# The context's norm, projections and delta rule beside the two feed-forwards

## The chip, the cores and the metric

The kernel runs on one core of one Trainium2 chip. The metric is the device time of one execution in microseconds (us). Matrix work runs on TensorE (PE in the profile, its weight loads PEld), elementwise work on VectorE (DVE) and ScalarE (ACT), a little on GpSimd (POOL); SyncE (SP) issues the DMAs. TensorE writes only to PSUM, which has eight banks of 128 x 512 float32.

## The reference

Two blocks on 256 tokens of width 1024, all in float32.

The first block has two layers. Each is a mixer (three branches, attention of two sorts and a convolution, gated and summed) and a feed-forward of width 4096:

```
h = rms_norm(x, g_ffn)
x = x + square(relu(h @ w_ff1)) @ w_ff2
```

The second block takes that x and a context of 256 tokens. Both are normalised, modulated by factors computed from two conditioning vectors, and multiplied by the same `w_in`. What matters here is that the context's part does not need x:

```
zx = modulate(rmsnorm(x,   g), mod_x) @ w_in     # needs the first block
zc = modulate(rmsnorm(ctx, g), mod_c) @ w_in     # does not
k_all, v_all = concat(kc, kx), concat(vc, vx)    # differential attention of qx
_, = wkv_scan(0, scan_c) -> s_ctx                # a delta rule over the context's 256 steps
y  = wkv_scan(s_ctx, scan_x)                     # and over x's, from the state it left
s = s * w - (s @ kk) (kk * a)^T + v k^T          # one step, per head, in two directions
```

The two branches are merged, and an expert stage (16384 experts, top 16 of 8 heads) follows.

## The kernel before

A matmul in float32 is made of three in the `fp32r` form: each operand is split into a high part (`wh`, `hh`, on ScalarE, line 304) and a low part (`wl`, `hl`, on VectorE, line 269), and lines 325 to 327 or 343 to 345 multiply high by high, low by high and high by low. Weights come by DMA as 128 x 1024 pieces (128 x 512 in the second block) into `raw`. A *unit* is 256 output columns of a projection: `linA_unit` gives them transposed, channels on the partitions, `linB_unit` tokens on the partitions; either is 48 matmuls of 256 columns. `bank()` hands out a PSUM bank: of `psa` (three) by default, `psw` (two) or `psr` (three) inside a `stream`, or the one bank of `psm` where the stream is `single`.

The stages, in the profile's time: mixer of layer 0, its feed-forward (313 to 512), mixer of layer 1, its feed-forward (819 to 1013), the second block (1013 to 1931), the experts. `layer()` holds mixer and feed-forward; both take their tiles from one pool, `layer`. The feed-forward runs 16 tiles: `f1` of tile i (line 893), relu and square (895 to 898), `f2` of tile i - 1 into four accumulating banks. At its last tile but one of layer 1 it computes the context's norm (`ctx_norm`) into `hh`, `hl`, and after the tiles the unit `zw` of the context (`w_proj`), of which the context uses one half of the columns.

`mods_stream` computes the modulation factors from the conditioning vectors in three rounds of eight steps; five steps run at the start of each feed-forward, and the first round, which the norms need, is complete there in layer 0 (line 1003).

`second()` then goes through this order of work:

```
z_proj(context): zk, zv, 8 units -> DRAM      front(context, half 0), back(context, half 0)
front(context, half 1); bk and bv of the context, 8 units; keys to DRAM
x to DRAM; norm of x; zw, zk, zv, zr of x     back(context, half 1), front(x, half 0)
bq, bk, bv, bg of x                           back(x, half 0), front(x, half 1)
attention                                     back(x, half 1); merges, output, norm
```

`wkv_front` makes, for half the heads, the decays (line 1231), the products of keys (line 1270), and inverts 32 x 32 triangular blocks on VectorE, going out to DRAM and back on both sides (`din`, `dout`; lines 1279 to 1303); its last part (1316, 1323) makes what the back takes. `wkv_back` carries the state S through eight groups of 32 steps (lines 1346, 1362, 1374). Their tiles come from two rotating sets: `w4` with 8 buffers and `w8` with 9. A front of the context takes 6 of `w8`, one of x 8 or 6.

What sets the order: each engine works through one queue in order. The queues are written at build time by a planner that simulates the program's timeline; among what is ready it prefers what stands earlier in the program, and `high_priority(offset=30000)` puts fronts and backs ahead of the projections. A tile that takes memory of another waits until the other is no longer used; this holds for the buffers of a rotating set and for a pool opened where another was closed.

Of the kernel before, what the change touches and what calls it, by code (L numbers as in the profile page):

```python
# [194 lines left out]
class Kern:  # L195
    def __init__(self, tc, A, flat_at, const_at, pack_at, out):
        self.tc, self.nc, self.A, self.at = tc, tc.nc, A, flat_at
        self.const_at, self.pack_at, self.out = const_at, pack_at, out
        self.n = 0
        self.ev = 0  # L200
        self.sfx, self.single = "", False
        self.every = 3
        self.last = None
        self.late = {}
        self.held = []
        self.wide = 2048
        self.piece = 1024

# [100 lines left out]
    def pieces(self, name, piece=None):  # L309

        off, n = self.at[name]
        piece = piece or self.piece
        raw = None if self.wide < n else self.load(name)
# [47 lines left out]
    def linA_unit(self, name, hh, hl, nk):  # L361
# [4 lines left out]
        for wh, wl in self.pieces(name):  # L366
            wh = wh.rearrange("p (j k c) -> p j k c", k=kk, c=128)
            wl = wl.rearrange("p (j k c) -> p j k c", k=kk, c=128)
            for i in range(wh.shape[1]):
# [4 lines left out]
                if k == 0:  # L374
                    m += 1
                    if m % 2 == 0:
                        yield ps
# [87 lines left out]
    def layer(self, l, pool):  # L465
# [5 lines left out]
        P = {k: pk[:, a:b] for k, (a, b) in at.items()}  # L471
# [407 lines left out]


        hh = self.t(self.work, [128, 8, T], "hh", F32R)
        hl = self.t(self.work, [128, 8, T], "hl", F32R)
        self.normT(self.halves(self.x), P["g_ffn"], hh, hl, spare="t")
        self.mods_units(5, self.last)
        with self.stream("t"):
            pw = [self.bank_pair(), [self.score_bank(), self.score_bank()]]
        prev = None
        for i in range(17):
# [13 lines left out]
            if i == 15 and l and self.more:  # L902
                self.ctx_front = self.ctx_norm(pool, "TG")
# [3 lines left out]
        if l and self.more:  # L907
            self.w_proj(pool, 0, *self.ctx_front)
        self.add_x(pw)

# [67 lines left out]
    def mods_stream(self):  # L978
# [10 lines left out]
        for r in range(3):  # L989
            ps = self.t(self.psm, [128, 512], "m")  # L990
            for k in range(8):
                for q in range(4):
                    if q % 2 == 0:
                        raw = self.t(self.lpool, [128, 1024], ("qk", "TG")[k % 2], bufs=4)
# [92 lines left out]
    def v_unit(self, pool, i, hh, hl, dst, kt):  # L1087
        a = self.t(pool, [128, 2, 256], "d2", bufs=4)
# [11 lines left out]
    def ctx_norm(self, pool, tag):  # L1100

        x = [self.t(pool, [128, D], tag, bufs=4) for t in range(2)]
        for t in range(2):
            self.nc.sync.dma_start(x[t], self.A["ctx"][128 * t:128 * t + 128])
        hh, hl = [self.t(self.work, [128, 8, T], n, F32R) for n in ("hh", "hl")]
        self.mod_norm(x, self.P2["norm1_g"], 0, 1, hh, hl)
        return hh, hl

    def w_proj(self, pool, src, hh, hl):
# [4 lines left out]
        for ps in self.linA_unit("zw0", hh, hl, 8):  # L1114
# [10 lines left out]
    def z_proj(self, pool, src, hh, hl, zd):  # L1125

        nc = self.nc
        for half in range(2):
            for n, base in (("zk", 8), ("zv", 16), ("zr", 0)):
                if n == "zr" and src == 0:  # L1130
                    continue
                for i in (2 * half, 2 * half + 1):
                    for ps in self.linA_unit(f"{n}{i}", hh, hl, 8):
                        o = self.t(pool, [128, 2, T], "d2", bufs=4)
# [195 lines left out]
    def wkv_back(self, state, S, od=None):  # L1330
# [92 lines left out]
        if self.dbg is not None:  # L1423
            nc.sync.dma_start(self.dbg["o_bx"].rearrange("(m p) t -> p m t", p=128)[:, m0:m0 + 4], o)
# [99 lines left out]
    def second(self, pool, xd):  # L1524
        nc, P = self.nc, self.P2
        self.rows2 = self.t(pool, [128, 384], "rows2")
        nc.sync.dma_start(self.rows2, self.A["rows2"].partition_broadcast(128))
        self.resets = self.t(pool, [128, 264], "resets")
# [9 lines left out]
        nc.vector.tensor_scalar(self.tmka, P["rw_k_a"], -1.0, 2.0, op0=ALU.mult, op1=ALU.add)  # L1538
        dram = lambda shape, name: self.t(self.dram, shape, name)
        kTd, qTd, vd = dram([128, 8, 512], "kTd"), dram([128, 8, T], "qTd"), dram([128, 4, 1024], "vd")  # L1540
        zc, zx = dram([128, 24, T], "zc"), dram([128, 24, T], "zx")
# [29 lines left out]
        back(st, S[:, 1])  # L1571
# [249 lines left out]
def body(tc, A, flat_at, const_at, pack_at, pk2_at, out, stop=None, dbg=None, skip=0):  # L1821
    nc = tc.nc
    with ExitStack() as ctx:
        K = Kern(tc, A, flat_at, const_at, pack_at, out)
        K.pk2_at, K.dbg = pk2_at, dbg
        K.setup(ctx)
        K.n4, K.n8 = 8, 9
# [5 lines left out]
        K.wad = K.t(K.dram, [128, T], "wad")  # L1833
        K.mods_pool = ctx.enter_context(pool("mods", bufs=1))
        pk = K.t(K.mods_pool, [128, A["pk2"].shape[1]], "pk2")
        K.P2 = {k: pk[:, a:b] for k, (a, b) in pk2_at.items()}
        with pool("xp", bufs=1) as K.xp:
# [5 lines left out]
            K.psa = ctx.enter_context(pool("psa", bufs=3, space=PSUM))  # L1843
# [3 lines left out]
            with pool("psm", bufs=1, space=PSUM) as K.psm, pool("psb1", bufs=2, space=PSUM) as K.psb:  # L1847
                with pool("small1", bufs=1) as K.small, pool("mtmp", bufs=1) as K.mtmp, pool("stage1", bufs=2) as K.stage, pool("late1", bufs=1) as late, pool("layer", bufs=1) as p:
                    K.late = {n: late for n in ("pk", "rows", "TG", "mt", "OT", "OL")}
                    K.tmp = p, [128, 512], "mt", F32, 4  # L1850
                    K.lpool, K.mstream, K.more = p, K.mods_stream(), stop is None or stop > 2
                    if skip < 2:
# [77 lines left out]
```

## Time and profile before

| | |
|---|---|
| median of 3 runs | 2844.91 us (2844.22 to 2846.0) |
| the profiled execution | 2839.05 us |
| its span, first to last instruction | 2837.1 us |
| TensorE busy | 2637.1 us, 93% |
| VectorE busy | 1977.8 us, 70% |
| ScalarE busy | 1424.6 us, 50% |
| DMA queue of SyncE | 50.4% of 16 engines' span |
| granted TensorE clock, mean | 0.939 of 2.4 GHz |

Times in the profile are counted from the first instruction, so the stages can be told by them. Busy time of TensorE is modelled, as matmuls are pipelined: a matmul's duration is longer than the distance to the next one, and busy shares of a stage say more than sums of durations. A group of instructions is named by its line, engine, operation and tiles, `out<-in`; many lines are those of helpers that all stages share.

### The profile page before, as it was taken

What the parts mean: (1) busy time and instruction counts of PE and PEld (TensorE: products, weight loads), DVE (VectorE), ACT (ScalarE), POOL (GpSimd) and SP (SyncE); (2) the same over time, 40 slices, a digit from 0 to 9 for tenths busy, and PEclk for the clock granted to TensorE, in tenths of its full rate; (3) what the DMA queues carried; (4) which work ended last, traced back from release to release, by engine and by line L of the source; (5) the groups of instructions that cost most, each with busy time, mean ns of one, the idle gap of its engine ahead of it and who ended that gap; (6) DMA issues with size and microseconds to landing.
All of it is one profiled execution on the core that took longest, in us unless ns stands there. A gap on an engine that the chain in (4) does not pass through costs nothing. (4 is left out here: it accounts for less than half of the span.)

```text
span 2837.1 us, 55078 instructions
## 1 busy us (share of the span) xinstructions
PE 2637.1 (93%) x21880; PEld 2314.7 (82%) x21880; DVE 1977.8 (70%) x4104; ACT 1424.6 (50%) x2417; POOL 13.1 (0%) x36
## 2 busy tenths in 40 slices
PE   7999999999999998899789785798989999999999
PEld 7987688898679997888777454688989998888887
DVE  6986555598675577887777766476886765666666
ACT  5554444555454455665454553345445654444444
POOL 0000000000000000000000000000000000000000
PEclk9999999999999998999897766599999999999999
DMA  5534755554376654644544212064554346666665
GB/s 189 181 140 142 285 194 189 169 168 142 119 259 189 189 190 133 180 150 144 157 130 141 84 37 80 12 207 159 182 182 145 124 142 203 207 216 214 210 216 185
DMA packets 214738, 467.16 MB, mean 165 GB/s; under 512 B 53072, under 2 KB 86608, under 8 KB 213968
## 3 DMA queue, kind: packets, MB, share of 16 engines
q1 hardware_dynamic: 214480, 463.64, 50.4%
q8 instruction: 172, 2.82, 0.4%
q14 instruction: 86, 0.70, 0.1%
HBM read 425.54 MB, written 38.01 MB: 163 GB/s over the span
## 5 line engine op out<-in xcount | busy, mean ns | idle before, releaser
L269 DVE TENSOR_TENSOR wl<-raw,wh 128x1024 fp32r<-128x1024 f32 (+2 forms) x726 | 732.4, 1013 | 379.2 <-ACT wh L304 370.6
L304 ACT ACTIVATE wh<-raw 128x1024 fp32r<-128x1024 f32 (+2 forms) x726 | 642.5, 890 | 691.5 <-PE a L326 316.2
L325 PE MATMUL a<-hh,wh 128*128 128x256 f32 x2784 | 797.8, 287 | 17.3 <-ACT wh L304 9.6
L327 PE MATMUL a<-hh,wl 128*128 128x256 f32 x2784 | 796.6, 287 | 9.1 <-DVE wl L269 8.8
L326 PE MATMUL a<-hl,wh 128*128 128x256 f32 x2784 | 794.5, 286 | 2.2 <-DVE hl L269 2.2
L325 PEld LDWEIGHTS a<-hh,wh 128*128 128x128 f32 x2784 | 533.8, 192 | 29.7 <-ACT wh L304 14.3
L327 PEld LDWEIGHTS a<-hh,wl 128*128 128x128 f32 x2784 | 533.0, 192 | 20.7 <-DVE wl L269 15.3
L326 PEld LDWEIGHTS a<-hl,wh 128*128 128x128 f32 x2784 | 533.6, 192 | 8.7 <-DVE hl L269 2.4
L344 PE MATMUL a<-wl,hh 128*128 128x256 f32 (+2 forms) x640 | 195.9, 307 | 15.6 <-DVE wl L269 15.1
L344 PE MATMUL b<-wl,ah 128*128 128x512 f32 x512 | 200.8, 392 | 0.0
L343 PE MATMUL a<-wh,hh 128*128 128x256 f32 (+2 forms) x640 | 192.9, 306 | 7.9 <-DVE hl L387 6.7
L343 PE MATMUL b<-wh,ah 128*128 128x512 f32 x512 | 191.1, 393 | 3.1 <-issue 3.1
L345 PE MATMUL b<-wh,al 128*128 128x512 f32 x512 | 192.0, 392 | 0.0
L345 PE MATMUL a<-wh,hl 128*128 128x256 f32 (+2 forms) x640 | 191.8, 301 | 0.0
L344 PEld LDWEIGHTS a<-wl,hh 128*128 128x128 f32 x640 | 127.0, 198 | 27.4 <-DVE wl L269 18.2
L260 ACT ACTIVATE w<-a 32x512 f32<-32x512 f32 (+1 forms) x168 | 99.3, 592 | 98.3 <-PE a L1362 43.2
L343 PEld LDWEIGHTS a<-wh,hh 128*128 128x128 f32 x640 | 127.7, 199 | 15.7 <-DVE hl L387 7.3
L1775 ACT ACTIVATE ah<-pact 128x256 fp32r<-128x256 f32 x128 | 52.7, 412 | 171.6 <-PE b L344 159.0
L345 PEld LDWEIGHTS a<-wh,hl 128*128 128x128 f32 x640 | 126.8, 198 | 4.0 <-issue 1.0
L269 DVE TENSOR_TENSOR wl<-rawv,wh 128x1024 fp32r<-128x1024 f32 x84 | 101.8, 1223 | 38.6 <-ACT wh L304 38.6
L269 DVE TENSOR_TENSOR al<-pact,ah 128x256 fp32r<-128x256 f32 x128 | 53.1, 423 | 89.8 <-ACT ah L1775 89.7
L827 DVE SCALAR_TENSOR_TENSOR z<-U,pk,z 128x256 f32<-128x256 f32 x240 | 114.9, 479 | 0.8
(515 smaller groups left out, 4325.7 us busy)
## 6 DMA issues: line engine op xcount, KB each, us to landing
raw<-in_flat SPq DMA_DIRECT2D x266, 512.0 KB, 4.3
raw<-in_peer SPq DMA_DIRECT2D x172, 512.0 KB, 3.9
raw<-in_flat SPq DMA_DIRECT2D x276, 256.0 KB, 3.5
rawv<-in_peer SPq DMA_DIRECT2D x84, 512.0 KB, 4.6
TG<-in_flat SPq DMA_DIRECT2D x28, 512.0 KB, 5.5
qk<-in_flat SPq DMA_DIRECT2D x24, 512.0 KB, 5.2
parked<-act SPq DMA_DIRECT2D x89, 128.0 KB, 2.0
pact<-parked SPq DMA_DIRECT2D x89, 128.0 KB, 4.2
```

The source lines that it names most:

```text
L260: nc.scalar.activation(out, in_, AF.Copy, scale=1.0 if scale is None else scale)
L269: self.nc.vector.tensor_tensor(out, a, b, op=ALU.subtract)
L304: self.nc.scalar.activation(h, src, AF.Copy)
L325: mm(ps, wh[:, k], xh[:, k], start=first and k == 0, stop=False)
L326: mm(ps, wh[:, k], xl[:, k], start=False, stop=False)
L327: mm(ps, wl[:, k], xh[:, k], start=False, stop=last and k == nk - 1)
L343: mm(ps, xh[:, k], wh[:, k], start=first and k == 0, stop=False)
L344: mm(ps, xh[:, k], wl[:, k], start=False, stop=False)
L345: self.last = mm(ps, xl[:, k], wh[:, k], start=False, stop=last and k == nk - 1)
L827: nc.vector.scalar_tensor_tensor(cv[:, c], U[:, c, k_:k_ + T], wd[:, k_:k_ + 1], cv[:, c], op0=ALU.mult, op1=ALU.add)
L1775: nc.scalar.activation(ah, act, AF.Copy)
```

## The change

The context's work leaves the second block, all but the keys of its attention (`bk`).

- `layer()` is cut in two: `mixer()` and `ffn()`, and each of the four gets a pool of its own, opened where the one before is closed. What has to last from mixer to feed-forward (`pk`, `rows`, `TG`, `mt`, `OT`, `OL`) was in a pool beside them already.
- In the first feed-forward, after its norm and the modulation's steps and ahead of its tiles in the program, `ctx_proj` computes the context's norm into two `w8` tiles, copies it to DRAM (`hcd`), and computes half of `zw`, the 8 units `zk` and `zv`, and the 4 units `bv`, with tiles of 128 x 1024.
- In each feed-forward, ahead of its tiles and at high priority, one half of the context's delta rule: `wkv_front` and `wkv_back` with 5 `w4` and 6 `w8` buffers, its PSUM banks `m` and `x` in turn, and its final S sent to DRAM (`Sd`).
- `psa` has two banks, `psx` one. Where `spare_bank` is set, the default stream takes `psx` at every third call; during the feed-forwards it is left to the delta rule, and the tiles have the two of `psa`.
- The modulation's weights come into `TG` (4 buffers) alone, no longer into `qk` and `TG`.
- The second block loads S and, during the last tiles of the second feed-forward, the context's `hh` and `hl` from DRAM. Its order begins with `bk` of the context (into a `w8` tile), x's norm, `zw` and z of x, and the rest of the context's keys; then `front(x, half 0)`. `w4` and `w8` have 8 and 9 buffers there as before.

```diff
     def bank(self):
+        if self.single == "c":
+            self.turn += 1
+            return self.t(*((self.psm, [128, 512], "m"), (self.psx, [128, 512], "x"))[self.turn % 2])
         if self.single:
             return self.t(self.psm, [128, 512], "m")
+        if not self.sfx and self.spare_bank:
+            self.turn += 1
+            if self.turn % 3 == 0:
+                return self.t(self.psx, [128, 512], "x")
...
+    def ffn(self, l, pool):
...
-        self.normT(self.halves(self.x), P["g_ffn"], hh, hl, spare="t")
+        self.normT(self.halves(self.x), self.P["g_ffn"], hh, hl, spare="t")
         self.mods_units(5, self.last)
+        self.spare_bank = False
+        if l == 0:
+            self.ctx_proj(pool)
+        with self.stream("n", "c"), self.tc.high_priority(offset=30000):
+            self.n4, self.n8 = 5, 6
+            tg = self.t(pool, [128, D], "TG", bufs=4)
+            self.wkv_consts(pool, tg[:, T:T + 264])
+            wa = tg[:, :T]
+            nc.sync.dma_start(wa, self.wad)
+            S = self.t(pool, [128, 2, 4, 64], "S")
+            nc.gpsimd.memset(S, 0.0)
+            self.wkv_back(self.wkv_front(pool, 0, l, self.zc, wa), S)
+            nc.sync.dma_start(self.Sd[l], S)
...
-            if i == 15 and l and self.more:
-                self.ctx_front = self.ctx_norm(pool, "TG")
+            if i == 15 and l:
+                self.ctx_front = [self.t(self.work, [128, 8, T], n, F32R) for n in ("hh", "hl")]
+                for n in range(2):
+                    nc.sync.dma_start(self.ctx_front[n].bitcast(F32), self.hcd[:, n])
...
-        if l and self.more:
-            self.w_proj(pool, 0, *self.ctx_front)
+        self.spare_bank = True
         self.add_x(pw)
+
+    def ctx_proj(self, pool):
+
+        nc = self.nc
+        x = [self.t(pool, [128, D], "TG", bufs=4) for t in range(2)]
+        for t in range(2):
+            nc.sync.dma_start(x[t], self.A["ctx"][128 * t:128 * t + 128])
+        hh, hl = [self.t(pool, [128, 8, T], "w8", F32R, bufs=6) for n in range(2)]
+        self.mod_norm(x, self.P2["norm1_g"], 0, 1, hh, hl)
+        for n, h in enumerate((hh, hl)):
+            nc.sync.dma_start(self.hcd[:, n], h.bitcast(F32))
+        self.w_proj(pool, 0, hh, hl)
+        self.z_proj(pool, 0, hh, hl, self.zc, "mt")
+        for i in range(4):
+            self.v_unit(pool, i, hh, hl, self.vd, 0, "mt")
...
     def second(self, pool, xd):
...
-        nc.gpsimd.memset(S, 0.0)
+        for hf in range(2):
+            nc.sync.dma_start(S[:, hf], self.Sd[hf])
...
-        wac = self.t(pool, [128, T], "wa0")
-        nc.sync.dma_start(wac, self.wad)
-        self.z_proj(pool, 0, hh, hl, zc)
...
-        st = front(0, 0, zc, wac)
-        back(st, S[:, 0])
-        st = front(0, 1, zc, wac)
-        a = self.t(self.xp, [128, 2, 16, 64], "xn", bufs=1)
+        self.n4, self.n8 = 8, 9
+        a = self.w8(pool, [128, 2, 16, 64])
         fc = self.da_front(pool, a, "bk", hh, hl)
-        for i, _ in enumerate(self.da_tail(pool, fc, self.rows2[:, 64:128], False, kTd, 0)):
-            self.v_unit(pool, i, hh, hl, vd, 0)
...
         self.z_proj(pool, 1, hh, hl, zx)
-        back(st, S[:, 1])
+        for _ in self.da_tail(pool, fc, self.rows2[:, 64:128], False, kTd, 0):
+            pass
         st = front(1, 0, zx, wax)
...
-            K.psa = ctx.enter_context(pool("psa", bufs=3, space=PSUM))
+            K.psa = ctx.enter_context(pool("psa", bufs=2, space=PSUM))
+            K.psx = ctx.enter_context(pool("psx", bufs=1, space=PSUM))
...
+                    for l in range(2):
+                        with pool(f"mixer{l}", bufs=1) as p:
+                            K.mixer(l, p)
+                        with pool(f"ffn{l}", bufs=1) as p:
+                            K.ffn(l, p)
```

`wkv_consts` holds the few constants of the delta rule that `second()` made; `w_proj` takes only the first half of the `zw` weights where its source is the context.

## Rows read from the trace of the kernel before

**Rows 1.** The page's first part: busy time of each engine over the span.
```profile
PE 2637.1 (93%) x21880; PEld 2314.7 (82%) x21880; DVE 1977.8 (70%) x4104; ACT 1424.6 (50%) x2417; POOL 13.1 (0%) x36
```

**Rows 2.** Busy time by stage; after POOL the granted clock, DMA share, GB/s.
```profile
core 0: us, PE busy (x) PEld busy (x) DVE busy (x) ACT busy (x) POOL busy (x), PEclk, DMA share, GB/s
313.00:512.00 199.00, 195.34 (x1238) 166.56 (x1237) 107.89 (x137) 92.20 (x115) 0.00 (x0) 1.00 0.62 217
819.00:1013.00 194.00, 188.65 (x1223) 166.24 (x1222) 116.24 (x176) 100.97 (x135) 0.00 (x0) 1.00 0.62 199
1013.00:1931.00 918.00, 777.71 (x9357) 669.00 (x9355) 659.42 (x1533) 474.29 (x931) 8.05 (x18) 0.83 0.41 127
1013.00:1540.00 527.00, 472.70 (x5773) 431.89 (x5771) 405.89 (x946) 289.58 (x525) 5.05 (x15) 0.93 0.51 156
1540.00:1700.00 160.00, 130.58 (x1224) 88.90 (x1224) 110.44 (x257) 91.11 (x222) 1.10 (x2) 0.68 0.21 63
1700.00:1842.00 142.00, 95.95 (x1832) 76.42 (x1835) 78.76 (x207) 50.48 (x108) 0.00 (x0) 0.61 0.17 46
1931.00:2837.00 906.00, 880.47 (x5847) 805.35 (x5846) 613.26 (x1183) 443.44 (x623) 0.62 (x1) 0.99 0.56 184
```

**Rows 3.** Single lines, in stretches: ns min/median/max, first and last start in us.
```profile
L1374 PE MATMUL a<-w,w x256: 218/218/268, 1206.4 to 1325.7; 64*64 64x64 f32 x128
...
L1374 PE MATMUL a<-w,w x256: 218/218/365, 1408.9 to 1509.5; 64*64 64x64 f32 x128
...
L1374 PE MATMUL a<-w,w x224: 218/311/367, 1594.8 to 1694.0; 64*64 64x64 f32 x112
...
L1374 PE MATMUL a<-w,w x224: 311/311/366, 1775.2 to 1826.2; 64*64 64x64 f32 x112
...
L1164 ACT ACTIVATE w<-w x4: 1044/1047/1057, 1057.0 to 1590.4; 128x1024 f32<-128x1024 f32 x4
...
L1164 ACT ACTIVATE w<-w x2: 1047/1052/1057, 1198.3 to 1405.9; 128x1024 f32<-128x1024 f32 x2
...
L1270 PE MATMUL a<-w,w x256: 211/219/240, 1243.7 to 1327.5; 64*64 64x32 f32 x128
...
L1270 PE MATMUL a<-w,w x256: 218/218/267, 1451.5 to 1526.1; 64*64 64x64 f32 x128
```

**Rows 4.** The timeline inside the second feed-forward: start and duration in us.
```profile
989.74 0.28 PE L327 MATMUL a<-hh,wl 128*128 128x256 f32 x1
...
990.09 0.28 PE L327 MATMUL a<-hh,wl 128*128 128x256 f32 x1
```

**Rows 5.** Groups of TensorE between 1013 and 1931, shapes kept apart: busy us, mean ns.
```profile
L1362 PE MATMUL a<-w,w 32*32 32x64 f32 x1024 | 63.0, 255 | 41.1 <-DMA w<-dout 21.7 <-DVE w L266 13.4 <-DVE w L1303 5.1
L1323 PE MATMUL a<-w,w 32*32 32x64 f32 x1024 | 40.2, 234 | 5.2 <-ACT w L260 4.6 <-issue 0.5
L1374 PE MATMUL a<-w,w 64*64 64x64 f32 x960 | 37.4, 263 | 8.2 <-ACT w L260 8.1
...
L1223 PE MATMUL a<-wa,wup 64*128 64x256 f32 x64 | 19.3, 424 | 0.4 <-ACT w L1228 0.4
...
L1270 PE MATMUL a<-w,w 64*64 64x32 f32 x512 | 15.3, 232 | 3.8 <-DVE w L263 3.7
L1346 PE MATMUL a<-S,w 64*32 64x64 f32 x512 | 14.0, 221 | 4.4 <-DVE S L263 3.4 <-DVE w L263 1.0
```

**Rows 6.** Groups of VectorE: splits at 313 to 512 and at 1134 to 1200.
```profile
L269 DVE TENSOR_TENSOR wl<-raw,wh 128x1024 fp32r<-128x1024 f32 x63 | 77.2, 1226 | 82.3 <-ACT wh L304 82.2
...
L269 DVE TENSOR_TENSOR wl<-raw,wh 128x512 fp32r<-128x512 f32 x27 | 18.4, 687 | 2.7 <-ACT wh L304 2.5
```

**Rows 7.** Single lines again: modulation, the first feed-forward's tiles, attention.
```profile
L1003 PE MATMUL m<-ident,mt x12: 272/273/332, 325.8 to 831.9; 128*128 128x128 f32 x12
...
L895 ACT ACTIVATE mt<-a x16: 578/582/582, 337.8 to 504.7; 128x512 f32<-128x512 f32 x16
...
L1448 PE MATMUL a<-d,dq x64: 589/1057/1220, 1540.7 to 1688.8; 64*128 64x512 f32 x64
```

**Rows 8.** DMA issues: how many, KB each, median us to landing.
```profile
zc<-d SPq DMA_DIRECT2D x8, 256.0 KB, 4.1
```

More of the change, by code (lines that the diff above doesn't have):

```diff
@@ L207, in __init__ @@
         self.piece = 1024
+        self.turn, self.spare_bank = 0, True
     def uid(self, s):
@@ L359, in linB_unit, with linA_unit @@
         return ps
-    def linA_unit(self, name, hh, hl, nk):
+    def linA_unit(self, name, hh, hl, nk, one=False):
         ps = None
@@ L365, in linA_unit @@
         m = k = 0
-        for wh, wl in self.pieces(name):
+        for wh, wl in self.pieces(name, part=128 * nk if one else None):
             wh = wh.rearrange("p (j k c) -> p j k c", k=kk, c=128)
@@ L375, in linA_unit @@
                     m += 1
-                    if m % 2 == 0:
+                    if m % 2 == 0 or one:
                         yield ps
@@ L462, in rope_rows, with mixer @@
         self.add(v, v, tmp)
-    def layer(self, l, pool):
+    def mixer(self, l, pool):
         nc, C = self.nc, self.C
@@ L470, in layer @@
         nc.sync.dma_start(pk, self.A[f"pk{l}"])
-        P = {k: pk[:, a:b] for k, (a, b) in at.items()}
+        P = self.P = {k: pk[:, a:b] for k, (a, b) in at.items()}
         rw = self.t(pool, [128, 320], "rows")
@@ L1113, in w_proj @@
         sg = self.t(pool, [128, T], "sgd") if src else None
-        for ps in self.linA_unit("zw0", hh, hl, 8):
+        for ps in self.linA_unit("zw0", hh, hl, 8, one=src == 0):
             self.shifted(wa, ps[:, 0], 24)
@@ L1818, in peer_experts, with body @@
                 nc.sync.dma_start(out[:, t, c], o)
[L1821 removed]
+def body(tc, A, flat_at, const_at, pack_at, pk2_at, out):
     nc = tc.nc
@@ L1833, in body @@
         K.wad = K.t(K.dram, [128, T], "wad")
+        K.zc = K.t(K.dram, [128, 24, T], "zc")
+        K.vd = K.t(K.dram, [128, 4, 1024], "vd")
+        K.hcd = K.t(K.dram, [128, 2, 8, T], "hcd")
+        K.Sd = [K.t(K.dram, [128, 2, 4, 64], f"Sd{n}") for n in range(2)]
         K.mods_pool = ctx.enter_context(pool("mods", bufs=1))
@@ L1847, in body @@
             with pool("psm", bufs=1, space=PSUM) as K.psm, pool("psb1", bufs=2, space=PSUM) as K.psb:
-                with pool("small1", bufs=1) as K.small, pool("mtmp", bufs=1) as K.mtmp, pool("stage1", bufs=2) as K.stage, pool("late1", bufs=1) as late, pool("layer", bufs=1) as p:
+                with pool("small1", bufs=1) as K.small, pool("mtmp", bufs=1) as K.mtmp, pool("stage1", bufs=2) as K.stage, pool("late1", bufs=1) as late:
                     K.late = {n: late for n in ("pk", "rows", "TG", "mt", "OT", "OL")}
-                    K.tmp = p, [128, 512], "mt", F32, 4
-                    K.lpool, K.mstream, K.more = p, K.mods_stream(), stop is None or stop > 2
-                    if skip < 2:
-                        for l in range(2 if stop is None else min(2, stop)):
-                            K.layer(l, p)
-                    if stop is None or stop > 2:
-                        for _ in K.mstream:
-                            pass
-                    if skip == 2:
-                        K.ctx_front = K.ctx_norm(p, "TG")
-                        K.w_proj(p, 0, *K.ctx_front)
+                    K.tmp = late, [128, 512], "mt", F32, 4
+                    K.lpool, K.mstream = late, K.mods_stream()
+                    for l in range(2):
[3 more added lines that the diff above has]
+                            K.ffn(l, p)
+                    for _ in K.mstream:
+                        pass
             K.late = {}
@@ L1863, in body @@
             K.stage = stage2.enter_context(pool("stage2", bufs=2, side="right"))
[L1864 to L1874 removed]
+            with pool("psr2", bufs=3, space=PSUM) as K.psr:
+                with pool("small2", bufs=1) as K.small, pool("late2", bufs=1) as late, pool("second", bufs=1) as p:
+                    K.late = {"d2": late}
+                    K.tmp = p, [128, 512], "d2", F32, 4
+                    K.nraw, K.nsplit, K.every, K.wide, K.piece = 6, 4, 1 << 30, 1024, 512
+                    K.second(p, xd)
+                    hh = K.t(K.work, [128, 8, T], "hh", F32R)
+                    hl = K.t(K.work, [128, 8, T], "hl", F32R)
+                    K.mod_norm(K.halves(K.x), K.P2["norm2_g"], 3, 0, hh, hl, spare="w")
             K.late = {}
@@ L1877, in body @@
             psw.close()
-            if stop is not None:
-                stage2.close()
-                nc.sync.dma_start(out.rearrange("(t p) d -> p t d", p=128), K.x)
-                return
             nc.sync.dma_start(x3d, K.x)
```

55 lines of the change are left out of this document (19 added, 36 removed).

## The prediction

> **What bounds the kernel now.** I read the page's first lines, then the busy time by stage, then where the chain of the four delta-rule passes starts and stops. TensorE is busy 2637 of 2837 us, 93% [rows 1], so work can hardly be hidden: what moves to another place costs TensorE time there. The stages show where TensorE's time is poor. In the two feed-forwards (313 to 512 and 819 to 1013) the granted clock is 1.00 and 195.3 of 199 and 188.7 of 194 us are busy. From 1013, the end of the second feed-forward, to 1931, where the expert stage starts, 777.7 of 918 us are busy: 140 idle, and the clock is 0.93 in the part with the projections (1013 to 1540) and 0.68 and 0.61 after it. The last stage, 880 of 906 busy at 0.99, is left alone by the change [rows 2].
>
> Why those 918 us are poor: four passes of the delta rule (`wkv_front`, then `wkv_back`; context half 0, context half 1, x half 0, x half 1) hang on one another. Line 1374, which only a back has, runs at 1206 to 1326, 1409 to 1510, 1595 to 1694 and 1775 to 1826; the fronts begin between 1057 and 1590, the third at 1406. The second half of a front (from line 1270 on) stands still until the back before it gives up its `w8` buffers: line 1270 is drawn out from 1244 to 1327, where the first back ends at 1326, and from 1452 to 1526, where the second ends at 1510 [rows 3]. So the four are one chain, and projections lie beside only its first part.
>
> **What moves.** Eight units `zk` and `zv` and four `bv`, 48 matmuls each; half of `zw` (24; the other half is computed today and not used); one norm; two passes. A 256-column matmul is issued every 0.117 us in the feed-forward (three in 0.35) [rows 4].
> - z: 384 x 0.117 = 45 us; v: 192 x 0.117 = 22; `zw` 3; the norm's 32 transposes 3. All in the first feed-forward: 73.
> - TensorE for one context pass: 7.7 and 7.0 (half of the two forms with 512 instructions, lines 1270 and 1346, that only the context has) and a quarter of lines 1362 (63.0), 1323 (40.2), 1374 (37.4) and 1223 (19.3, and as much for 1224): 59.5 [rows 5]. Small matmuls overlap in the array and part of these rows ran at the low clock; some smaller groups are left out. I take 58, with 45 and 70 as the ends.
> - VectorE: a pass is at most what 1013 to 1540 shows: 406 us [rows 2] less some 200 splits of 512 columns at 0.69 us [rows 6] = 268, for two and a half passes: 107. First feed-forward: 108 + 25 splits at 1.23 [rows 6] = 31 + 15 for the shifts + 107 = 261 of some 350 us; second 116 + 107 = 223 of 268. ScalarE, 92 and 101 [rows 2], is lower. The DMAs (12.5 MB of weights, the turns through DRAM) find the queue at 0.62. I cost all this at nothing beside TensorE; where that cover fails, it is the late pass of rival 3.
>
> **First feed-forward.** TensorE: 199 + 73 + 58 = 330. Stalls: where passes and projections are mixed today, 54 of 527 us are idle [rows 2], 10%, with two and a half passes in them; for one pass in 330 I take 6%, 20 us (bounds 0 and 33). Growth 73 + 58 + 20 = 151. Is the pass in time? The modulation's last transposes come at 326; the norm takes about 16 (the feed-forward's own, with its first 48 matmuls, fills 313 to 338); `zw` and four z units 26 [rows 7]; out to DRAM and back two DMAs of 4 us [rows 8]: the front starts at 376. A front took 149 (1057 to 1206), a back 101 to 120 [rows 3]: end at 626 to 645, while TensorE has work until 512 + 151 = 663. TensorE decides, by 20 us. That margin matters: the next mixer's tiles now take the same memory and wait for the pass.
>
> **Second feed-forward.** TensorE: 194 + 58 + 14 of stalls = 266. The pass has its z at hand: 4 + 149 + 101 to 120 = 254 to 273. A tie; I take 268, growth 74 (bounds 50 and 100).
>
> **From there to the experts (918 today).** Two bounds.
> - The chain: context `bk` beside x's norm 25, `zw`, six z units and the trip through DRAM 50, the front's first half 46 (1406 to 1452), its second 85 (1510 to 1595), back 99, the second half of the last front 81 (1694 to 1775), back 51, and 105 from 1826 to 1931 [rows 3]: 542.
> - TensorE: 777.7 less 624 matmuls of z, v and `zw` at 0.125 (between the 0.117 and what the idle moments between them add) = 78, less two passes, 116: 584 busy at today's mixture of clocks, and idle from nothing to today's 140: 584 to 724.
>
> I take 600, close to the lower end of the second. Attention (line 1448, 1541 to 1689 [rows 7]) would fall beside the x half-1 front and back, where 46 of 142 us are idle today, at a clock of 0.61 [rows 2]: most of that idle is filled, and the clock can gain. Gain 918 - 600 = 318 (bounds 194 and 376).
>
> On the clock: the rows show 0.61 for a stretch with little but a bare pass, 0.93 for passes mixed with projections and 1.00 for dense feed-forward matmuls [rows 2], between levels of 1.2 and 2.4 GHz. The Trainium skill (TensorE: Matmul & The Clock Gate, A second HAM failure mode: psum-queue depth-cycling) has a rule that speaks against the change: turning through PSUM banks makes TensorE pause so often that its clock swings between the levels. By that rule the swing would come into the feed-forwards; it is rival 2, and the row at 0.93 agrees with it that far.
>
> **Sum.** 151 + 74 - 318 = -93 on the profiled execution's 2839: 2746. The runs' median, 2844.9, is 6 higher: 2752. This case's own range is 2705 to 2800.
>
> **Rivals.**
> 1. All fits better. Passes cost 45, stalls next to nothing, the last block follows its chain: growth 73 + 45 + 5 and 50, last block 560, -185 at the best; with half of the difference, 2706 and below. For it: the chain's 542. Against: 584 busy. Chance 0.17.
> 2. The clock swings in the feed-forwards, because the pass has two PSUM banks in turn (`m`, `x`) and the tiles two of their own where they had three. At 0.93 their 620 us take 47 more: 2799. For it: that row. Against: dense bursts of feed-forward matmuls lie between. Chance 0.12.
> 3. The other side: the pass outlasts the feed-forward. It has 5 and 6 buffers where it had 8 and 9, two banks, and stands behind splits of 1024 columns. At the longest front and back of today (1198 to the next back at 1409: 211; 120 for the first back [rows 3]) the first feed-forward ends at 376 + 331 = 707, not 663, and the second takes 335, not 268, since mixer and last block wait for its memory: 111 more, 2863. The change turns into a loss once the two overruns pass 93 us together, 46 a pass. Against: that front was so long because it waited for a back's buffers. Chance 0.12, of which 0.04 for an overrun that just eats the gain and ends within 0.2%.
> 4. The work only changes its place: the last block keeps its 140 idle, 724; 225 - 194 = +31, 2876. For it: TensorE at 93%. Against: the idle belongs to a chain that loses half its links. Chance 0.07.
> 5. The change doesn't do what it says: the order written at build time puts the pass behind the tiles, not beside them. Two bare passes of 250, less the 144 of TensorE and stalls already counted: +356, some 3108. Against: passes and projections are interleaved that way today. Chance 0.02.
>
> Faster 0.79 (the forecast 0.50, rivals 1 and 2); within 0.2%, about what a timing of this kernel can tell from no change, 0.04; slower 0.17. The range goes down to 2685, into rival 1, and up to 2840, which takes in rival 2 and stops short of rival 3.
>
> **What would show it.** Line 1374 in two clusters inside the feed-forwards, the first ending before the last line-895 tile, and two after them; the first feed-forward some 350 us long, the second 268, clock 1.00; the next mixer starting within a few us of the last add to x; then 600 us to the experts, with a clock above 0.68 under attention. Wrong if the mixer or the last block waits for `w4` or `w8` memory, if the spacing of matmuls in the feed-forward rises well over 0.117, or if the idle of 1700 to 1842 survives.

## The result, and the profile after

The changed kernel takes 2797.9 us in the median of 4 runs (2794.3 to 2799.6), the kernel before 2845.5 on the same chip: a ratio of 0.983, 95% interval 0.981 to 0.985, or 48 us gained where 93 were forecast. The profiled span falls from 2837.1 to 2796.9, by 40: the profiled execution of the kernel before was 6 us faster than its median. The page's first part, beside [rows 1]: TensorE has kept its busy time and its share has grown by a point. Hardly any of its work was saved; the 40 us are idle time that is gone.

```profile
PE 2635.9 (94%) x21856; PEld 2293.4 (82%) x21856; DVE 1978.4 (71%) x4085; ACT 1423.3 (51%) x2392; POOL 14.2 (1%) x45
```

The busy time by stage, to be read against [rows 2] (first feed-forward, second mixer, second feed-forward, second block up to x's first delta-rule front, from there to the experts, the last stage):

```profile
320.00:662.00 342.00, 326.43 (x3199) 282.12 (x3198) 236.96 (x416) 179.79 (x259) 1.55 (x4) 0.97 0.59 192
662.00:986.00 324.00, 313.13 (x2198) 258.61 (x2196) 243.17 (x545) 159.60 (x313) 2.39 (x9) 0.97 0.51 166
986.00:1232.00 246.00, 241.99 (x2263) 200.81 (x2262) 171.74 (x290) 128.91 (x181) 1.54 (x4) 0.99 0.56 173
1232.00:1357.00 125.00, 100.96 (x997) 95.49 (x997) 81.61 (x203) 59.56 (x112) 0.64 (x5) 0.82 0.51 163
1357.00:1894.00 537.00, 476.92 (x5281) 396.44 (x5279) 390.46 (x908) 294.42 (x599) 4.23 (x6) 0.83 0.44 136
1894.00:2797.00 903.00, 877.63 (x5848) 802.50 (x5847) 613.67 (x1184) 443.72 (x624) 0.61 (x1) 0.99 0.58 184
```

Set against the terms of the sum, in us of span:

| | before | after | forecast growth | measured |
|---|---|---|---|---|
| start of the first feed-forward | 313 | 320 | 0 | +7 |
| first feed-forward | 199 | 342 | +151 | +143 |
| second mixer | 307 | 324 | 0 | +17 |
| second feed-forward | 194 | 246 | +74 | +52 |
| second block, to x's first front | 393 | 125 | -318 | -268 |
| second block, from there | 525 | 537 | 0 | +12 |
| last stage | 906 | 903 | 0 | -3 |
| sum | 2837 | 2797 | -93 | -40 |

The forecast of 600 for the block named 75 for the part ahead of x's front, 318 below the 393 of before, which leaves 525 for the rest. The marks of before are those of [rows 3], and its busy time between them is

```profile
1013.00:1406.00 393.00, 351.32 (x4083) 325.02 (x4082) 307.98 (x714) 222.25 (x410) 3.85 (x12) 0.93 0.53 161
1406.00:1931.00 525.00, 426.39 (x5276) 343.99 (x5275) 351.44 (x820) 252.04 (x522) 4.20 (x6) 0.76 0.33 102
```

After the change the block is 662: 578 us of TensorE's time in it, where 584 were forecast, and 84 idle, where 16 were.

The two stretches behind x's front, 525 and 537, do not hold the same work. The first matmul of each group of three, by its two lines (325 and 343 before, 333 and 351 after; `a` and `x` are banks):

```profile
L325 PE MATMUL a<-hh,wh 128*128 128x256 f32 x256 | 78.3, 306 | 1.7 <-ACT hh L1594 1.1 <-ACT wh L304 0.6
L343 PE MATMUL a<-wh,hh 128*128 128x256 f32 x31 | 9.4, 302 | 0.0
```
```profile
L333 PE MATMUL a<-hh,wh 128*128 128x256 f32 x211 | 63.1, 299 | 4.1 <-ACT hh L1621 4.1
L351 PE MATMUL a<-wh,hh 128*128 128x256 f32 x144 | 42.6, 296 | 1.9 <-DVE d L1137 1.8
L333 PE MATMUL x<-hh,wh 128*128 128x256 f32 x112 | 32.6, 291 | 0.2 <-ACT d L268 0.2
L351 PE MATMUL x<-wh,hh 128*128 128x256 f32 x48 | 14.4, 299 | 0.8 <-ACT d L268 0.8
```

That is 287 groups before and 515 after. 228 groups, about 14 units, that lay ahead of x's front before now lie behind it; in exchange the last back of the context is gone from there. Idle time in that stretch falls from 99 to 60 us and the clock rises from 0.76 to 0.83, but TensorE's time rises from 426 to 477.

Single lines of the changed kernel: its line 1404 is the old 1374 (once in every step of a back), 918 the old 895 (the feed-forward's tiles), 1194 the old 1164 (where a front begins), and 1198 is a front's first matmul.

```profile
L1404 PE MATMUL x<-w,w x128: 218/218/267, 546.3 to 664.4; 64*64 64x64 f32 x128
...
L1404 PE MATMUL m<-w,w x128: 218/218/365, 1174.3 to 1261.3; 64*64 64x64 f32 x128
...
L918 ACT ACTIVATE mt<-a x16: 577/597/602, 450.3 to 653.9; 128x512 f32<-128x512 f32 x16
...
L918 ACT ACTIVATE mt<-a x16: 572/580/602, 1015.7 to 1223.0; 128x512 f32<-128x512 f32 x16
...
L1198 PE MATMUL m<-consts,w x16: 170/251/251, 1020.2 to 1021.8; 128*128 128x2 f32 x16
...
L1194 ACT ACTIVATE w<-w x2: 1043/1044/1046, 1356.7 to 1524.1; 128x1024 f32<-128x1024 f32 x2
```

Both passes lie beside the tiles. The first ends 10 us after its last tile, the second 38. The second's front began at 940, when the load of z had landed, and TensorE took up its first matmul at 1020, after the matmuls and transposes of the modulation that share its bank `m` (the last of them at 1016). Its last steps stand bare. TensorE's wait and the row of that stretch:

```profile
PE x L351 <- ACT wh L312: 11.2, 1, 11.2
```
```profile
1232.00:1290.00 58.00, 37.45 (x483) 33.02 (x482) 28.05 (x84) 18.51 (x35) 0.64 (x5) 0.68 0.35 113
```

37 of 58 us busy at a clock of 0.68: the end of a pass, then 11 us until the block's first weights are split, and from 1273 on the first matmuls of `bk`. SyncE's queue shows what looks like the reason: the store of the state waits at its head for the pass to end, and the block's weight loads stand behind it.

```profile
SPq L907 <- DVE S L271: 26.9, 1, 26.9
```

### The profile page after: what moved, and what is told of

The parts are those of the page before. It is cut to its first block, busy times and chain, and to the rows that moved or that the text cites. A ratio compares the mean times of both kernels' runs of the same rounds, so it can differ in the third digit from the quotient of the medians.

```text
span 2796.9 us, 54976 instructions
## 1 busy us (share of the span) xinstructions
PE 2635.9 (94%) x21856; PEld 2293.4 (82%) x21856; DVE 1978.4 (71%) x4085; ACT 1423.3 (51%) x2392; POOL 14.2 (1%) x45
## 4 chain that ended last, share of the span: by engine, by line
PE 79%; DVE 10%; DMA 6%; ACT 4%; issue 2%; SPq 0%; DVEq 0%; ACTq 0%
PE a L333 8%; PE a L335 8%; PE a L334 8%; PE b L353 4%; PE b L351 4%; PE b L352 4%; PE b L1767 3%; PE x L335 3%; PE x L333 3%; PE x L334 3%; PE a L352 3%; PE a L351 3%; PE a L353 3%; DVE wl L277 3%; DMA raw<-in_peer 2%
## 5 line engine op out<-in xcount | busy, mean ns | idle before, releaser
L312 ACT ACTIVATE wh<-raw 128x1024 fp32r<-128x1024 f32 (+1 forms) x701 | 638.2, 913 | 689.3 <-PE a L334 247.4
L277 DVE TENSOR_TENSOR wl<-raw,wh 128x1024 fp32r<-128x1024 f32 (+1 forms) x701 | 727.4, 1041 | 357.9 <-ACT wh L312 332.6
L333 PE MATMUL a<-hh,wh 128*128 128x256 f32 x1920 | 550.2, 287 | 8.8 <-ACT hh L1621 4.1
L335 PE MATMUL a<-hh,wl 128*128 128x256 f32 x1920 | 549.5, 286 | 4.5 <-DVE wl L277 4.2
L334 PE MATMUL a<-hl,wh 128*128 128x256 f32 x1920 | 547.2, 285 | 0.6 <-DVE hl L277 0.5
L333 PEld LDWEIGHTS a<-hh,wh 128*128 128x128 f32 x1920 | 365.5, 190 | 22.0 <-ACT wh L312 4.9
L334 PEld LDWEIGHTS a<-hl,wh 128*128 128x128 f32 x1920 | 364.9, 190 | 5.4 <-DVE hl L277 0.7
L333 PE MATMUL x<-hh,wh 128*128 128x256 f32 x720 | 205.8, 286 | 5.6 <-ACT wh L312 5.2
L335 PE MATMUL x<-hh,wl 128*128 128x256 f32 x720 | 206.6, 287 | 3.0 <-DVE wl L277 3.0
L334 PE MATMUL x<-hl,wh 128*128 128x256 f32 x720 | 204.9, 285 | 0.0
```

Of the source, the lines that this page charges most:

```text
L277: self.nc.vector.tensor_tensor(out, a, b, op=ALU.subtract)
L312: self.nc.scalar.activation(h, src, AF.Copy)
L333: mm(ps, wh[:, k], xh[:, k], start=first and k == 0, stop=False)
L334: mm(ps, wh[:, k], xl[:, k], start=False, stop=False)
L335: mm(ps, wl[:, k], xh[:, k], start=False, stop=last and k == nk - 1)
```

## The experiments

Theory: passes and projections cost what was forecast, and the lost 46 us (2798 against 2752) are the second pass's overrun, through bank `m` and the store in SyncE's queue. Rival: the block is long by itself, and the passes gave back less than they were charged with.

**The two passes left out, in the changed kernel (`no_passes`) and in the kernel before (`before_no_passes`).** The state stays zero; the passes' computation is missing. In the first:
```
-            self.wkv_back(self.wkv_front(pool, 0, l, self.zc, wa), S)
+            if l not in (0, 1):
+                self.wkv_back(self.wkv_front(pool, 0, l, self.zc, wa), S)
```
and in the second the two `front(0, ...)` and two `back` calls of the context are taken out.

> Both context passes are left out (S stays zero; wrong state for x); projections, norm and loads stay. What the passes cost where they are now. By TensorE's sum alone, 2 x 58: 2682. With the stalls of the prediction, 72 each: 2654. If each also delays what follows (17 us in the second mixer, 38 us ahead of the second block): 2627.

> The kernel before, without the two context passes (S stays zero): what they cost in the old place. If they are links of a chain that sets the end: x's first pass no longer waits until 1510 for its second half but gets there at about 1240 to 1290, so -220 to -270, 2575 to 2625. If only TensorE's sum counts: -116, 2729. The difference between this price and that of no_passes is what the move of the passes alone is worth; the prediction has 318 - 78 = 240 against 144, so about 96 less what the projections lose.

2660.4 us, ratio to the kernel before 0.937 (0.934 to 0.941), and 2650.2, ratio 0.932 (0.929 to 0.936). By these ratios the passes cost 131 us beside the feed-forwards and 193 in the second block: the move of the passes gains 62, with an uncertainty of some 15, where the sum had 88 (240 in the block, 152 beside the feed-forwards). The rest of the change (the projections above all, with the modulation's tiles, the banks and the pools) is a loss of 15 (0 to 30) where the sum had a gain of 5. Of the expectations, the first came out nearest to the one with stalls (2 x 72), and the second between its two: 193 where the chain had 220 to 270 and TensorE's sum 116. The stages of the first (the two feed-forwards with the mixer between them, then the block), and of the second:

```profile
316.00:609.00 293.00, 275.89 (x1853) 240.38 (x1852) 164.58 (x241) 135.83 (x180) 1.16 (x5) 0.98 0.65 218
609.00:924.00 315.00, 302.86 (x2138) 255.22 (x2137) 243.04 (x544) 158.70 (x311) 1.57 (x5) 0.98 0.50 164
924.00:1121.00 197.00, 193.77 (x1214) 166.52 (x1213) 108.36 (x140) 92.35 (x114) 0.43 (x2) 0.99 0.59 194
1121.00:1757.00 636.00, 554.99 (x5928) 473.04 (x5927) 460.01 (x1079) 347.29 (x698) 5.11 (x11) 0.86 0.46 142
```
```profile
314.00:513.00 199.00, 196.51 (x1238) 167.10 (x1237) 107.91 (x138) 92.07 (x114) 0.00 (x0) 0.99 0.65 217
513.00:830.00 317.00, 309.63 (x2139) 261.41 (x2138) 240.51 (x538) 156.41 (x307) 0.97 (x2) 0.95 0.48 155
830.00:1026.00 196.00, 191.28 (x1235) 167.98 (x1234) 118.70 (x181) 102.08 (x136) 0.00 (x0) 1.00 0.59 196
1026.00:1750.00 724.00, 627.94 (x6547) 551.43 (x6546) 512.56 (x1169) 386.72 (x770) 5.67 (x12) 0.88 0.48 146
```

The row that decides is the block at 1121: with no context pass anywhere it is still 636 us, with 81 idle, and in the second kernel 96 are idle. So more than half of the 140 idle us of before does not need the context's passes to be there, and moving the passes could not bring the block to 600. Two smaller readings: projections and norm add 94 us to the first feed-forward (293 against 199), pass 0 another 49.

**The projections moved, the passes left in the block (`proj_only`).**
```
-            self.wkv_back(self.wkv_front(pool, 0, l, self.zc, wa), S)
+            if l not in (0, 1):
+                self.wkv_back(self.wkv_front(pool, 0, l, self.zc, wa), S)
...
+        st = front(0, 0, self.zc, wac)
+        back(st, S[:, 0])
+        st = front(0, 1, self.zc, wac)
...
+        back(st, S[:, 1])
```

> The context's norm and its z, v and zw projections run beside the first feed-forward as in the changed kernel, but both passes of the delta rule stay in the second block, in the order that the kernel before has. Theory A (moving the projections gains the block about as much as it costs the first feed-forward and the mixers, and the whole gain comes from the passes): 2830 to 2850 us. Rival B (the projections carry part of the gain, about half): 2805 to 2822 us. Rival C (they alone are a loss of over 20 us): 2865 us or more.

2909.4 us, ratio 1.023 (1.018 to 1.029): 66 us slower than before, so rival C. First feed-forward and block:

```profile
319.00:611.00 292.00, 277.16 (x1854) 240.26 (x1853) 164.71 (x242) 135.90 (x179) 1.16 (x5) 0.97 0.66 219
...
1126.00:2009.00 883.00, 760.63 (x8719) 635.60 (x8718) 613.33 (x1435) 435.46 (x856) 8.02 (x18) 0.77 0.38 114
```

The projections cost the first feed-forward 93 us and give the block 35 (918 to 883): they had lain beside the passes, and without them the passes stand bare (clock 0.77 over the block, 122 idle). Against `no_passes` the two bare passes cost 0.086 of 2845, 245 us. That is about the 240 that the sum charged. Each part alone would mislead: the passes are worth 193 as long as the projections cover them and 245 after, the projections 35 while the passes are there and 88 (724 to 636) without them.

**The second pass alone left out (`no_pass1`).** Same edit with `l not in (1,)`.

> The changed kernel without the second of the two context passes (its half of the state stays zero, that part of the computation is left out). Theory A (this pass outlasts the feed-forward's tiles and costs the second block its start): the second feed-forward falls from 246 to about 190 us and the second block from 662 to 610 to 625 us, so 85 to 100 us less than the changed kernel. Rival B (a pass costs only the TensorE time that it adds, and the second block is long for another reason): 55 to 62 us less, the block still at 655 us or more.

2718.5 us, ratio 0.956 (0.951 to 0.960): 78 us below the changed kernel by the ratios, between the two expectations (second feed-forward, way to x's front, and from there):

```profile
988.00:1184.00 196.00, 192.70 (x1211) 165.51 (x1210) 107.68 (x139) 92.16 (x114) 0.43 (x2) 0.99 0.58 195
1184.00:1273.00 89.00, 82.78 (x648) 80.81 (x647) 67.05 (x171) 51.90 (x100) 0.55 (x5) 0.94 0.61 195
1273.00:1823.00 550.00, 490.91 (x5285) 401.72 (x5284) 393.04 (x913) 295.17 (x603) 4.62 (x6) 0.82 0.43 133
```

The pass adds 50 us to the feed-forward and 36 to the way from there to x's front (125 against 89), 86 together; forecast were 72. The stretch behind x's front does not shrink (550 against 537). So the overrun is real but small, and 89, not 75, is what that way takes with no overrun at all.

**Is it the start of the pass, or SyncE's queue?** Six versions of the changed kernel move these. `mods_late` puts all of modulation round 3 behind the pass:
```
-            if i == 14 and l == 0:
-                self.mods_units(3)
+            if i == 14:
+                self.mods_units(8 if l else 3)
```
(with none of round 3 at the second mixer's end or ahead of the feed-forward); `early_pass` puts it all at the mixer's end and has the store on GpSimd's queue, `store_pool` has only that (`nc.gpsimd.dma_start(self.Sd[l], S)`), `pool_queue` also the passes' loads of z and of `wup`; `mods_late_store` and `combo` are `mods_late` with the edits of `store_pool` and of `pool_queue`.

> The modulation's third round (8 steps) is moved from the end of the second mixer and the start of the second feed-forward to its 15th tile, behind the pass; nothing is left out. Theory A: the pass beside the second feed-forward starts late (first matmul of line 1198 at 1017, 31 us into the stage) because that round holds PSUM bank m until then, and so overhangs the tiles: its first matmuls come at 945 to 990, its end moves from 1262 to before the last tile (about 1232), the second block's first matmuls from 1273 to about 1240, total 2798 - 33 = 2765. Rival B: memory and the DMA queue set the start of pass and second block; the pass gets the bank earlier and nothing else moves, 2790 to 2800. Rival C: only TensorE's sum counts, which is the same: 2793 to 2803.

> The loads of zc and wup for the context's passes and the store of S are issued from GpSimd's queue in place of SyncE's; the program is otherwise the same. Theory A: SyncE's queue stands still behind them, 24.1 us at line 1183 (911 to 936, the second mixer's end starves for weights) and 26.9 us at line 907 (the first weights of the second block land only after the pass): mixer 2 from 324 to about 310, the gap between the last step of the pass (1262) and the first bk matmul (1273) closes; total 2798 - 25 = 2773. Rival B: the weights' own buffers lie in memory that the pass still uses, so they cannot come sooner, and only the mixer gains: 2780 to 2787. Rival C: neither queue matters: within 5 us of 2798.

> All eight steps of the modulation's round 3 are run at the end of the second mixer, none at the start of the second feed-forward, and the store of the state is issued by GpSimd's queue instead of SyncE's. Theory A (the second pass ends after the feed-forward's tiles because its first matmul waits until 1017 us for the PSUM bank that the modulation holds, and the store of the state at the head of SyncE's queue holds up the second block's first loads): the second mixer grows by about 17 us, the pass starts at about 950 and ends before the last tile, the second feed-forward is about 229 us and the second block 590 to 623 us from norm to norm: about 2752 us, 40 below the changed kernel. Rival B (the second block's length goes by how its units happen to fall, and the first loads wait for memory in any case): 2785 to 2800 us, the block at 640 us or more.

> Only the store of the state moves to GpSimd's queue. Theory A (27 us of SyncE's queue behind that store hold up the second block's first weights): the block's first projection starts about 10 to 15 us earlier, 2783 to 2788 us. Rival B (the load of the up-projection's weights, hoisted to the head of the same queue, waits there for the memory of the state's tile just as long): within 5 us of the changed kernel.

> Modulation round 3 behind the second pass (at the second feed-forward's tile 15, as in mods_late), and the store of the state on GpSimd's queue. Theory A (mods_late lost in the feed-forward what it gained in the block because SyncE's queue stood 26 us at the store of the state with the modulation's and the last tile's weights behind it): the second feed-forward 265 to 275 instead of 298 us, the block as in mods_late, 2760 to 2772 us. Rival B (the work of the modulation has to be done somewhere, and TensorE decides): 2785 us or more.

> As mods_late_store, with the loads of z and of the up-projection's weights for the two passes on GpSimd's queue as well. Theory A (these loads, waiting at the head of SyncE's queue, cost the second mixer's end 4 us and the feed-forward 7): 8 to 12 us below mods_late_store. Rival B (no place where SyncE's queue waits sets the end): within 4 us of mods_late_store.

| | us | ratio to before | second feed-forward + way to x's front | from there |
|---|---|---|---|---|
| changed kernel | 2797.9 | 0.983 (0.981 to 0.985) | 246 + 125 = 371 | 537 |
| `mods_late` | 2791.9 | 0.983 (0.979 to 0.987) | 298 + 78 = 376 | 525 |
| `early_pass` | 2811.7 | 0.989 (0.985 to 0.994) | 244 + 124 = 368 | 553 |
| `store_pool` | 2811.3 | 0.988 (0.984 to 0.993) | 243 + 125 = 368 | 560 |
| `pool_queue` | 2818.4 | 0.992 (0.989 to 0.995) | 239 + 132 = 371 | 562 |
| `mods_late_store` | 2823.1 | 0.992 (0.989 to 0.994) | 301 + 79 = 380 | 557 |
| `combo` | 2816.2 | 0.990 (0.986 to 0.993) | 300 + 81 = 381 | 552 |

The kernels were timed in several rounds on different chips, so the ratios are what can be compared. None is faster than the changed kernel: `mods_late` is level with it, `pool_queue` and `mods_late_store` are slower. In `mods_late` the pass did start at 943 and end at 1233, before the tiles, and the modulation and the last tile then stood where the overrun had been: 298 and 78 us in place of 246 and 125. In `early_pass` the pass started at 1016 all the same: the modulation, though it stands earlier in the program, held bank `m` to 1013, so this run did not test what it was built for. The store's wait is gone from SyncE's queue in `store_pool`, and another stands at its head, the block's load of `wup`, which the planner has put ahead and which waits for the memory of the state's tile. In `mods_late_store` it is a load of the modulation that waits for bank `m`:

```profile
SPq L1246 <- DMA Sd<-S: 29.4, 1, 29.4
```
```profile
SPq L1035 <- PE m L1036: 28.4, 2, 27.8
```

From the start of the feed-forward to x's front these kernels take 368 to 381 us, wherever the longest wait of SyncE's queue, 26 to 34 us in each, is placed. Theory A of `mods_late`, `store_pool`, `pool_queue` and `mods_late_store` is refuted by their times. For `combo` it stays undecided: it is 6 us below `mods_late_store` by the ratios, with an uncertainty of some 12, where theory A had 8 to 12 and its rival at most 4. So the wait read above as a reason is not shown to cost anything; but as another took its place each time, no run is free of such a wait either.

What did move is the stretch behind, 525 to 562 us with the same work. Its idle time is 60 to 71 us in all seven; what differs is TensorE's busy time, 460 us at a clock of 0.88 in `mods_late`, 477 at 0.83 in the changed kernel and 486 to 494 at 0.82 or 0.83 in the five with a GpSimd store. The order of the instructions is worked out at build time, and one DMA on another queue changes TensorE's order too, so these versions are not clean one-edit tests of that stretch. Each row is also one execution, and those of the kernel before spread from 2829 to 2856 us in these rounds. Why all five with a GpSimd store have the stretch longer stays open.

**The attention left out (`no_attn`).**
```
-        for h in range(8):
+        nc.vector.memset(O, 0.0)
+        nc.vector.memset(ss, 1.0)
+        for h in range(0):
```

> The changed kernel without the head loop of the second block's attention (scores, exponentials, transposes, values: that part of the computation is left out, its output is set to zero). The loop holds 84 us of TensorE's time between 1600 and 1790 us, much of it at a granted clock of 0.56. Theory A (the 534 us from x's first delta-rule front to the final norm are TensorE's work at the lowered clock, so that time under the passes is not free): 45 to 80 us less than the changed kernel, the stretch at 455 to 490 us. Rival B (the chain of x's two passes sets the end, and the attention lies beside it): less than 20 us less, the stretch at 515 us or more.

2761.2 us, ratio 0.971 (0.967 to 0.975): 34 us below the changed kernel, the stretch (by the marks of the expectation) at 497, between the two theories. Of the attention's 84 us on TensorE 34 show; the other 50 lie beside x's passes. From x's front to the experts, without the attention:

```profile
1354.00:1855.00 501.00, 423.29 (x5029) 369.93 (x5028) 355.75 (x811) 252.29 (x473) 4.23 (x6) 0.81 0.44 135
```

78 us are idle here and 60 with the attention, so it fills 18 us of idle time. The last front's second half and the last back, in the changed kernel and here:

```profile
1623.00:1710.00 87.00, 67.16 (x997) 45.80 (x998) 68.99 (x181) 44.46 (x103) 0.95 (x1) 0.77 0.32 83
1710.00:1790.00 80.00, 73.70 (x788) 52.94 (x791) 38.91 (x106) 40.42 (x111) 0.00 (x0) 0.56 0.12 39
```
```profile
1619.00:1697.00 78.00, 55.05 (x886) 45.63 (x884) 55.41 (x139) 25.27 (x45) 0.95 (x1) 0.52 0.23 59
1697.00:1751.00 54.00, 41.25 (x638) 31.88 (x638) 20.39 (x51) 17.20 (x38) 0.00 (x0) 0.50 0.01 2
```

Bare, these two links take 78 and 54 us, about the 81 and 51 of the prediction's chain; with the attention 87 and 80. So it is the back that gets longer under the attention, on a TensorE busy 74 of 80 us. The clock does rise with the attention, from 0.52 to 0.77 and from 0.50 to 0.56, but under the back it stays near the lower level.

**The modulation's tiles (`before_tg`).** The kernel before with one line of the change:
```
-                        raw = self.t(self.lpool, [128, 1024], ("qk", "TG")[k % 2], bufs=4)
+                        raw = self.t(self.lpool, [128, 1024], "TG", bufs=4)
```

> The kernel before, with one line of the change alone: all raw tiles of the modulation's weights take turns in the four TG buffers instead of in four TG and four qk. Theory A (this is what makes each mixer of the changed kernel 7 to 8 us later, since TensorE waits for TG's DMA): the first feed-forward starts at about 320 instead of 313 us, the second mixer takes about 314 instead of 307, the whole is 10 to 20 us longer. Rival B (the mixers' growth comes from the memory that the passes and projections hold): within 4 us of the kernel before.

2859.9 us, ratio 1.006 (1.004 to 1.008): 16 us slower, as theory A has it. By stages the first feed-forward starts at 315, not 320, and the mixer takes 314, as expected. The line alone could account for the 15 us that the rest of the change costs. But `before_no_passes`, in which that line and the mixers are those of before, has a mixer of 317: a new order at build time moves a mixer by as much. So that 16 us come with the line is measured, that the four buffers fewer are their mechanism is not.

## Why the prediction was right in sign and twice too large

- **First feed-forward, +151: right** (+143). Projections, norm and idle time came to 94 (73 and the 20 of stalls: 93), the pass to 49 (58). The stalls had been charged for the pass among the projections; `no_passes` shows them without it, so that these two terms fit as well as they do is in part luck. The pass was in time but for 10 us.
- **Rival 2, the clock in the feed-forwards: refuted.** In the two stretches where tiles and pass are mixed the clock is 1.00, though the pass turns through two banks. The rule of the Trainium skill that was weighed (TensorE: Matmul & The Clock Gate, A second HAM failure mode: psum-queue depth-cycling) works through TensorE's pauses between groups of matmuls. This trace shows no swing there, but hardly any pauses either (1.0 of 250 and 0.1 of 150 us idle), so it does not test the rule. The row at 0.93 that was said to agree with it had 54 of 527 us idle [rows 2].

```profile
400.00:650.00 250.00, 248.99 (x2643) 219.69 (x2642) 179.67 (x276) 135.55 (x181) 1.12 (x2) 1.00 0.55 174
1050.00:1200.00 150.00, 149.87 (x1539) 130.15 (x1538) 118.88 (x183) 85.26 (x115) 1.11 (x2) 1.00 0.58 168
```

- **Second feed-forward, +74 ("A tie; I take 268"): too high by 22**, because the pass outlasts the tiles and its end falls into the block, which is rival 3 in small. The pass ended 276 us into the stage, near the 254 to 273 of the forecast; it was the tiles that were done sooner. Together with the way to x's front, 343 were forecast and 371 measured: 14 more for the pass (`no_pass1`: 86, not 72) and 14 more for the way (89, not 75).
- **The step that failed: "I take 600, close to the lower end of the second", that is, 16 us of idle time in the block.** It took 662, with 84 idle. TensorE's time fits (584; 578), in part by luck: the 578 hold the end of the second pass, and without a pass there the same work takes 555 (`no_passes`) to 574 (`no_pass1`). The expectation that "most of that idle is filled, and the clock can gain" was right in direction and too large: behind x's front idle time fell from 99 to 60 us and the clock rose from 0.76 to 0.83, with some 14 units more beside x's passes. The attention fills 18 us of idle time and shows 34 of its 84; under it the last back takes 80 us at 0.56, where it took 51 [rows 3]. Rival 4's answer, "the idle belongs to a chain that loses half its links", fails: with no context pass at all 81 us stay idle, 74 of them behind x's front. Of the 84, 24 lie ahead of x's front, where the pass's end and the wait behind it stand, against 7 in `no_passes`; the other 60 lie behind it, where 59 and 74 stay idle in `no_pass1` and `no_passes`. Whether they belong to x's own two passes no run shows: they are spread over many waits, the longest 11 us.
- **The mixers, costed at nothing: +24.** "The next mixer's tiles now take the same memory" was named and not priced, and the change of the modulation's tiles was not costed at all. That line alone makes the kernel before 16 us slower, but the two marks, the start of the first feed-forward and the second mixer, grow by 2 and 7 with it, 9 of the 24. How much of the rest is memory and how much order is open.
- In sum: -8 for the first feed-forward, +28 to x's front, +12 behind it, +24 for the mixers, -3 in the last stage: 53 between -93 and -40.

## What to carry to other kernels

Idle time in a stage with several chains need not belong to the chain that is moved: before counting it as a gain, ask how much of it the kernel would have with that chain gone altogether (here 81 to 96 of 140 us). Two things that cover each other have no price of their own (the passes were worth 193 or 245 us, the projections 35 or 88), so a sum over both has to be made in an order: the first at its price beside the other, the second at its price alone. A long wait at the head of a DMA queue is not yet a cost: in five versions that took the store out of it another wait of 28 to 34 us stood there, and none was faster.

## What had not been expected

- Kernels with the same work in a stretch differ there by as much as many edits are worth: x's stretch took 525 to 562 us in seven of them, and an untouched mixer 307 or 317. The order worked out at build time differs between them; how much of the spread it makes, beside that from one execution to the next, no run separates.
- The granted clock differs too. The last back took 72 us at 0.69 in `mods_late`, and 80 at 0.56 in the changed kernel:

```profile
1707.00:1779.00 72.00, 65.70 (x764) 45.62 (x764) 37.95 (x103) 40.75 (x111) 0.00 (x0) 0.69 0.13 43
```
- Under a bare pass the clock is at the lower of its two levels (0.50 of full speed, 1.2 of 2.4 GHz, in `no_attn`), though TensorE is busy 41 of 54 us; small matmuls of the same kind, those of the context's passes among the feed-forward's tiles, run at 1.00.
